# Small products in fewer bursts in the attention and the scan of a hybrid layer

## The chip, the core and the metric

The kernel runs on one core of a Trainium2 chip. The metric is the time on the device in microseconds (us), lower is better; a kernel is run several times and the median counts. The engines of the core work side by side, each through its own list of instructions in order: TensorE (PE in the profile; its weight loads are PEld), VectorE (DVE), ScalarE (ACT), GpSimd (POOL) and SyncE (SP), which issues transfers. An instruction that needs what another engine makes waits on a semaphore, and all that stands behind it in its list waits with it.

## What is computed

One layer over 2048 tokens of width 1024 and 16 learned meta tokens. One combined projection feeds two branches. Branch A is a gated DeltaNet (8 heads of 128, chunks of 64 in the reference, 128 in the kernel); branch B is a sliding-window attention in which four query heads share each of four key heads, over the own chunk of 64, the two before it and the meta tokens.

```python
def step(S, inp):                                   # branch A, the scan over chunks
    u_c, w_c, attn_c, q_c, k_c, gl_c = inp
    v_new = u_c - jnp.einsum('bhik,bhkv->bhiv', w_c, S)
    o_c = jnp.einsum('bhik,bhkv->bhiv', q_c, S) + jnp.einsum('bhij,bhjv->bhiv', attn_c, v_new)
    S = S * gl_c[..., None, None] + jnp.einsum('bhik,bhiv->bhkv', k_c, v_new)
    return S, o_c
...
scores = jnp.einsum('bkgncd,bknsd->bkgncs', q, k_w).astype(f32) * (SWA_HD ** -0.5)   # branch B
scores = scores - slopes[:, :, None, None, None] * dist
probs = jax.nn.softmax(jnp.concatenate([scores, sink], axis=-1), axis=-1)[..., :-1]
o = jnp.einsum('bkgncs,bknsd->bkgncd', probs.astype(v_w.dtype), v_w)
...
y_a = o_a * silu(z_a)                               # after a root mean square norm per head
y_b = o_b * silu(z_b)
mixed = g_a * (y_a @ w_proj_a) + g_b * (y_b @ w_proj_b)
return layer_norm(DEEPNORM_ALPHA * h + mixed @ w_out, ln_w, ln_b)
```

## The kernel before

The tokens are worked through in four blocks of 512. The bulk of the work is the projections: for each unit of 128 output columns a function issues 24 big products (L311, 128 x 512) into one bank of PSUM; the products use a high and a low part of the data and of the weights, which ScalarE (L275, the cast) and VectorE or GpSimd (L146, the difference) make from each weight tile.

Between the big products stands everything else. After six big products a projection yields; `run()` then advances a clock by one *tick* and gives each of two streams at most one step, at the rates in `RATES` and `SIDE`. A unit is thus four ticks. The stream `chain` holds the scan of four head groups (`stage_c`) and then the attention (`swa()`); `side` prepares the groups (decays, the key products of `stage_b1`, the triangular inverses). A step that has a tail (an evaluation that waits for another engine) hands it to `bg()`, a heap of background tasks: `yield 2` in a task lets it go on two ticks later, and a tick releases the due tasks ahead of the streams' steps. The order of each engine's list comes from this and from nothing else. On TensorE the small products of a step so form a *burst* between big ones.

The attention works through 16 items a block (key head `kv`, a pair of chunks `cp2`):

- `swa_front` issues eight score products (L1105), four operations on VectorE that add the position penalty and keep the minimum (L1107, each followed by a row that reads the accumulator), and m2, the sink's share (L1110). A background task does the exponentials on ScalarE two ticks later (L1117, L1119), and three ticks after these the normalisation on VectorE: sum L1121, reciprocal L1122, four scalings L1126.
- `swa_turn(ch, w)` transposes the probabilities of one of two chunks (L1140); ScalarE copies them out, rounded, as the high part (L1142), and a tick later VectorE makes the low part (L1147).
- `swa_vals(ch, w)` multiplies them with the values (L1156, L1158 with the low part, L1159). `swa_out` adds the two halves of the result (ScalarE L1164, VectorE L1165) and gates it into `zs` (L1169, two operations).

The front of the next item is issued one step ahead of the transposes of an item, and an item's second value products and its output (`late`) in the steps of the next one. In the scan, per chunk: the product of keys and state (L971), then the right-hand side, the triangular solve, `wd` (L984), its product into the state; `out` multiplies the chunk's attention matrix with `wd` (L960), adds (L962) and squares (L965). At the end a reciprocal square root of the square sums (L1001 and the helper lines L160 to L169), eight scales (L1006), and the output transposes of `stage_y` (L1023).

## Time and profile before

| | us |
|---|---|
| median of 3 runs (2647.66 to 2649.97) | 2648.5 |
| the profiled execution's own time | 2648.3 |
| its span, first to last instruction | 2646.5 |
| TensorE busy | 2608.6 (99%) |
| VectorE busy | 1533.4 (58%) |
| ScalarE busy | 1222.9 (46%) |
| GpSimd busy | 772.8 (29%) |

Durations below come from the profiled execution. A matmul's end is modelled in it and neighbouring matmuls overlap, so what a product adds is read from the start of one to the start of the next, or from the chain that ended last. x4 in a row is a group of four neighbouring instructions of one kind. The mean granted clock of TensorE was 0.998 of full speed.

### The profile page before, as it was taken

How to read it: one execution, taken by the hardware profiler on the slowest of the kernel's cores; microseconds unless marked ns; L12 is line 12 of the kernel's file. 1: busy time of each engine (PE TensorE's matmuls, PEld its weight loads, DVE VectorE, ACT ScalarE, POOL GpSimd, SP SyncE). 2: the span in 40 equal slices, each digit the busy share in tenths (PEclk: the TensorE clock that was granted, in tenths of full speed). 3: DMA queues.
4: the chain of work that ended last, by engine and by line, in shares of the span. 5: the costliest groups of instructions: out<-in, count | busy, mean ns of one | idle time of the engine just before them, and what ended most of it. 6: DMA issues, size and time to landing. Idle time of an engine off the chain costs nothing.

```text
span 2646.5 us, 44333 instructions
## 1 busy us (share of the span) xinstructions
PE 2608.6 (99%) x15444; PEld 2173.8 (82%) x15444; DVE 1533.4 (58%) x3863; ACT 1222.9 (46%) x3260; POOL 772.8 (29%) x1792
## 2 busy tenths in 40 slices
PE   9999999999999999999999999999999999999998
PEld 7677878888888888888888888888888888888886
DVE  6667756763565554763465554676347456476435
ACT  4565545552245544653224554565323454365422
POOL 2554333532056330111116532010102753011022
PEclk9999999999999999999999999999999999999999
DMA  7655555653675454674466545476347644557533
GB/s 257 207 198 180 186 191 159 200 167 96 205 244 169 135 167 143 201 207 132 152 225 186 170 135 164 151 212 184 120 157 243 190 142 149 164 172 210 171 98 136
DMA packets 243136, 461.61 MB, mean 174 GB/s; under 512 B 77648, under 2 KB 135760, under 8 KB 242912
## 3 DMA queue, kind: packets, MB, share of 16 engines
q1 hardware_dynamic: 242912, 458.78, 54.4%
q8 instruction: 122, 2.00, 0.3%
q14 instruction: 102, 0.84, 0.1%
HBM read 379.87 MB, written 78.81 MB: 173 GB/s over the span
## 4 chain that ended last, share of the span: by engine, by line
PE 89%; DVE 6%; ACT 3%; DMA 1%; issue 1%; SPq 0%; POOL 0%; DVEq 0%; ACTq 0%
PE acc L311 63%; PE ps L1140 2%; PE ps L1105 2%; PE ps L915 1%; PE ps L960 1%; PE ps L807 1%; PE ps L971 1%; PE ps L1158 1%; PE ps L992 1%; PE acc L1408 1%; PE acc L1411 1%; PE acc L1410 1%; PE ps L979 1%; PE ps L981 1%; PE ps L1408 1%; PE ps L1411 1%
## 5 line engine op out<-in xcount | busy, mean ns | idle before, releaser
L311 PE MATMUL acc<-xh,wh 128*128 128x512 f32 x1800 | 735.2, 408 | 0.3 <-ACT wh L275 0.3
L311 PE MATMUL acc<-xl,wh 128*128 128x512 f32 x1800 | 705.4, 392 | 0.0
L311 PE MATMUL acc<-xh,wl 128*128 128x512 f32 x1800 | 480.7, 397 | 0.0
L275 ACT ACTIVATE wh<-wr 128x1024 fp32r<-128x1024 f32 (+1 forms) x246 | 258.4, 1050 | 281.6 <-PE acc L311 151.8
L311 PEld LDWEIGHTS acc<-xh,wh 128*128 128x128 f32 x1800 | 339.1, 188 | 60.1 <-issue 1.4
L311 PEld LDWEIGHTS acc<-xl,wh 128*128 128x128 f32 x1800 | 339.7, 189 | 57.1
L311 PEld LDWEIGHTS acc<-xh,wl 128*128 128x128 f32 x1800 | 329.1, 189 | 65.6 <-issue 0.5
L718 DVE SCALAR_TENSOR_TENSOR s<-st,cw,s 128x512 f32<-128x512 f32 x288 | 229.4, 797 | 108.2 <-ACT st L713 101.2
L311 PE MATMUL acc<-y,wh 128*128 128x512 f32 x1024 | 251.5, 392 | 0.0
L146 DVE TENSOR_TENSOR wl<-wr,wh 128x1024 fp32r<-128x1024 f32 (+2 forms) x125 | 161.9, 1295 | 149.7 <-ACT wh L275 128.6
L841 POOL TENSOR_TENSOR tm<-X,g 128x60 f32<-128x60 f32 (+24 forms) x496 | 163.1, 329 | 251.8 <-DMA g<-d 216.7
L311 PEld LDWEIGHTS acc<-y,wh 128*128 128x128 f32 x1024 | 188.5, 188 | 36.7
L311 PE MATMUL acc<-xh,wr 128*128 128x512 f32 x624 | 210.7, 402 | 0.0
L1257 POOL TENSOR_TENSOR g<-g 128x512 f32<-128x512 f32 x32 | 69.7, 2177 | 395.4 <-DVE g L1250 385.5
L843 POOL TENSOR_TENSOR X<-X,tm 128x60 f32<-128x60 f32 (+24 forms) x496 | 170.8, 344 | 38.8
L1142 ACT ACTIVATE s<-ps 104x512 fp32r<-104x512 f32 (+2 forms) x128 | 76.3, 597 | 153.3 <-PE ps L1140 137.3
L1250 DVE SCALAR_TENSOR_TENSOR g<-g,acc 128x512 f32<-128x512 f32 x64 | 44.0, 687 | 154.5 <-PE acc L311 154.5
L311 PEld LDWEIGHTS acc<-xh,wr 128*128 128x128 f32 x624 | 115.6, 188 | 21.5
L311 PE MATMUL acc<-y,wl 128*128 128x512 f32 x512 | 130.7, 392 | 0.0
L146 POOL TENSOR_TENSOR wl<-wr,wh 128x256 fp32r<-128x256 f32 x120 | 87.0, 756 | 137.4 <-ACT wh L275 116.6
L760 POOL TENSOR_TENSOR g<-cm,gh 128x256 fp32r<-128x256 f32 x64 | 53.9, 872 | 249.6 <-DVE gh L672 206.9
L1241 ACT ACTIVATE g<-acc,bg__162 128x512 f32<-128x512 f32 x64 | 44.1, 689 | 177.3 <-PE acc L311 171.0
(340 smaller groups left out, 4679.6 us busy)
## 6 DMA issues: line engine op xcount, KB each, us to landing
wr<-in_wfm_dram SPq DMA_DIRECT2D x214, 512.0 KB
wl<-ws SPq DMA_DIRECT2D x165, 512.0 KB
wr<-ws SPq DMA_DIRECT2D x78, 512.0 KB
wh<-ws SPq DMA_DIRECT2D x75, 512.0 KB
ws<-wl SPq DMA_DIRECT2D x68, 512.0 KB
g<-kd SPq DMA_DIRECT2D x240, 96.0 KB
ws<-wh SPq DMA_DIRECT2D x38, 512.0 KB
wr<-in_wo_dram SPq DMA_DIRECT2D x32, 512.0 KB
```

Source lines behind the costliest of these rows:

```text
L146: eng.tensor_tensor(out=out_, in0=src, in1=f(hi), op=ALU.subtract)
L275: A.activation(hi[:, k], raw[:, k], AF.Copy)
L311: T.matmul(ps, w_[:, k, :], r_(k), start=(n == 0), stop=(n == 3 * NK - 1))
L718: V.scalar_tensor_tensor(out=acc, in0=st[:, 3 - d:TB + 3 - d], scalar=cw[:, s, 3 - d:4 - d], in1=acc, op0=ALU.mult, op1=ALU.add)
L760: G.tensor_tensor(out=gt[:, hh, c:c + 2], in0=tri.unsqueeze(1).to_broadcast([P, 2, P]), in1=part[:, c:c + 2, h0 + hh:h0 + hh + 1].to_broad ...
L841: G.tensor_tensor(out=tm[:, :n, :r], in0=X[:, :n, j:j + 1].to_broadcast([P, n, r]), in1=L[:, j:j + 1, j + 1:].to_broadcast([P, n, r]), op= ...
L843: G.tensor_tensor(out=X[:, :n, j + 1:], in0=X[:, :n, j + 1:], in1=tm[:, :n, :r], op=ALU.add)
L1105: T.matmul(o_, d["q", rt][:, 2 * cp2 + ch], KX[:, l, ch, s:208], start=l == 0, stop=l == 1)
L1140: T.transpose(out=pT[0:kt, j * 256 + rt * P:j * 256 + rt * P + P], in_=Pt[:, ch, rt, s + j * kt:s + j * kt + kt], identity=ident)
L1142: A.activation(ph[0:kt], pT[0:kt], AF.Copy)
L1257: G.tensor_tensor(out=m[:, u % 2, :], in0=t[:, 0, :], in1=t[:, 1, :], op=ALU.add)
L1408: T.matmul(acc, ah, wl[:, k2, :], start=False, stop=kq == 3 and k2 == 1)
```

## The change

In the attention an item has three steps in place of five: the first transposes and the late value products of the item before go in one step, the second transposes and the first value products in another; the low part counts as ready a tick later. In the scan the product of `out` is issued in the step that starts the next chunk, behind the product of keys and state, and the last one ahead of the attention. The key products of `stage_b1` form two bursts instead of one, the output transposes wait three ticks instead of one, a meta triangle's first step one tick more; two copies of the meta keys stand ahead of the differences. A rate changes from 1.20 to 1.00. The numbers of small and of big products are the same.

```diff
--- before.py
+++ after.py
@@ -44,7 +44,7 @@
 
 GS = (26, 9)
 NG = 6
-RATES = (0.45, 0.45, 0.45, 0.50, 1.20)
+RATES = (0.45, 0.45, 0.45, 0.50, 1.00)
 SIDE = (0.60, 0.50, 0.50, 0.55, 0.35)
 
 
@@ -398,10 +398,11 @@
     def meta_kb(u):
         def go(pf):
             for i in range(2):
+                for a in (0, 64):
+                    A.activation(kmt[a:a + 64, 0, 2 * u + i, :], pf[64 * i:64 * i + 64, :NM], AF.Copy)
+            for i in range(2):
                 kv = 2 * u + i
                 src = pf[64 * i:64 * i + 64, :NM]
-                A.activation(kmt[0:64, 0, kv, :], src, AF.Copy)
-                A.activation(kmt[64:128, 0, kv, :], src, AF.Copy)
                 for a in (0, 64):
                     V.tensor_tensor(out=kmt[a:a + 64, 1, kv, :], in0=src, in1=f(kmt[64 * i:64 * i + 64, 0, kv, :]), op=ALU.subtract)
         return go
@@ -490,7 +491,7 @@
             for hh in range(2):
                 T.matmul(pz[:NM, hh * NM:hh * NM + NM], M[:, lv, hh, :], W[:, 1, hh, :], start=True, stop=True)
             A.activation(Z, pz[:NM, 0:32].rearrange("p (h i) -> p h i", h=2), AF.Copy)
-            yield 2
+            yield 2 + (g == 0)
             n = 2 if lv < 3 else 1
             pw = bank()
             for hh in range(2):
@@ -800,19 +801,20 @@
             yield from until(lambda: "E" in d)
             E = d["E"]
             yield
-            pks = [bank() for hh in range(2)]
-            for hh in range(2):
-                for c in range(NC4):
-                    kc = kT[:, hh, c * P:(c + 1) * P]
-                    T.matmul(pks[hh][:, c * P:(c + 1) * P], kc, kc, start=True, stop=True)
             V.tensor_scalar(out=sk, in0=sk, scalar1=4e-6, scalar2=None, op0=ALU.add)
             V.reciprocal(out=cj, in_=sk)
             V.tensor_tensor(out=cj, in0=cj, in1=beta[:, :, h0:h0 + 2].rearrange("p c h -> p h c"), op=ALU.mult)
             V.tensor_scalar(out=ncj, in0=cj, scalar1=-1.0, scalar2=None, op0=ALU.mult)
             V.tensor_tensor(out=ce, in0=cj, in1=eg[:, 1, :, h0:h0 + 2].rearrange("p c h -> p h c"), op=ALU.mult)
             for hh in range(2):
+                pk = bank()
                 for c in range(NC4):
-                    V.scalar_tensor_tensor(out=LT[:, hh * NC4 + c, :], in0=pks[hh][:, c * P:(c + 1) * P], scalar=ncj[:, hh, c:c + 1],
+                    kc = kT[:, hh, c * P:(c + 1) * P]
+                    T.matmul(pk[:, c * P:(c + 1) * P], kc, kc, start=True, stop=True)
+                if hh:
+                    yield
+                for c in range(NC4):
+                    V.scalar_tensor_tensor(out=LT[:, hh * NC4 + c, :], in0=pk[:, c * P:(c + 1) * P], scalar=ncj[:, hh, c:c + 1],
                                            in1=E[:, hh, c * P:(c + 1) * P], op0=ALU.mult, op1=ALU.mult)
             d.update(ktok=ktok, LT=LT, sk=sk, cj=cj, ce=ce)
             bg(inverse(g))
@@ -954,21 +956,27 @@
             so = tiny([P, 2, NC4], "so")
 
             def out(c, wd):
-                yield 2
-                pks = bank()
+                po = bank()
                 for hh in range(2):
-                    T.matmul(pks[:, hh * P:hh * P + P], attn[:, hh, c, :], wd[:, 0, hh, :], start=True, stop=True)
-                yield 2
-                V.tensor_tensor(out=o[:, :, c, :], in0=pks[:, 0:256].rearrange("p (h d) -> p h d", h=2), in1=o[:, :, c, :], op=ALU.add)
-                yield 1
-                for hh in range(2):
-                    A.activation(junk, o[:, hh, c, :], AF.Square, accum_out=so[:, hh, c:c + 1])
-                d["so", c] = True
-
+                    T.matmul(po[:, hh * P:hh * P + P], attn[:, hh, c, :], wd[:, 0, hh, :], start=True, stop=True)
+
+                def end():
+                    yield 2
+                    V.tensor_tensor(out=o[:, :, c, :], in0=po[:, 0:256].rearrange("p (h d) -> p h d", h=2), in1=o[:, :, c, :], op=ALU.add)
+                    yield 1
+                    for hh in range(2):
+                        A.activation(junk, o[:, hh, c, :], AF.Square, accum_out=so[:, hh, c:c + 1])
+                    d["so", c] = True
+
+                bg(end())
+
+            wd = None
             for c in range(NC4):
                 pks = bank()
                 for hh in range(2):
                     T.matmul(pks[:, hh * P:hh * P + P], kT[:, hh, c * P:(c + 1) * P], S[g][:, hh, :], start=True, stop=True)
+                if c:
+                    out(c - 1, wd)
                 R = s2([P, 2, P])
                 for hh in range(2):
                     V.scalar_tensor_tensor(out=R[:, hh, :], in0=pks[:, hh * P:hh * P + P], scalar=neg[:, c, h0 + hh:h0 + hh + 1],
@@ -993,8 +1001,8 @@
                 for hh in range(2):
                     V.scalar_tensor_tensor(out=S[g][:, hh, :], in0=S[g][:, hh, :], scalar=eg[:, 2, c, h0 + hh:h0 + hh + 1],
                                            in1=pu[:, hh * P:hh * P + P], op0=ALU.mult, op1=ALU.add)
-                bg(out(c, wd))
                 yield
+            out(NC4 - 1, wd)
 
             def end():
                 yield lambda: ("so", NC4 - 1) in d
@@ -1014,7 +1022,7 @@
 
             d = gr[g]
             yield lambda: ("ok", "zs", 1) in d
-            yield 1
+            yield 3
             o, zs = d["o"], d["zs"]
             gr[g] = None
             for hh in range(2):
@@ -1145,6 +1153,7 @@
                 yield 1
                 pl = s2([P, 512], F32R)
                 V.tensor_tensor(out=pl[0:kt], in0=pT[0:kt], in1=f(ph[0:kt]), op=ALU.subtract)
+                yield 1
                 w["p", ch] = kt, ph, pl
 
             bg(end())
@@ -1209,13 +1218,11 @@
                     yield
                 yield from until(lambda: w["n"])
                 swa_turn(0, w)
-                yield
                 if late is not None:
                     late()
-                    yield
-                swa_turn(1, w)
                 yield
                 yield from until(lambda: ("p", 0) in w and ("ok", "zs", 1) in sr[kv])
+                swa_turn(1, w)
                 w["pO"] = bank()
                 swa_vals(0, w)
                 yield
```

What this does to the order of instructions at three places, from the two programs' printed order; a name's number tells one buffer from another. TensorE, block 2, attention before: two of the four score rows of an item (ps_12746; its probabilities will be g_12735), six big products, and the first transposes of the item before, whose probabilities are g_12615.

```order
L1105 MATMUL ps_12746<-g_12596,g_11697 128x208 x2
L1105 MATMUL ps_12746<-g_12596,g_11823 128x208 x2
L311 MATMUL acc_12760<-xh_7832,wh_12650 128x512
L311 MATMUL acc_12760<-xl_7833,wh_12650 128x512
L311 MATMUL acc_12760<-xh_7832,wh_12650 128x512
L311 MATMUL acc_12760<-xl_7833,wh_12650 128x512
L311 MATMUL acc_12760<-xh_7870,wh_12650 128x512
L311 MATMUL acc_12760<-xl_7871,wh_12650 128x512
L1140 MATMUL ps_12767<-cm,g_12615 104x128 x4
L311 MATMUL acc_12760<-xh_7870,wh_12650 128x512
```

After, at the same item:

```order
L1113 MATMUL ps_13281<-g_13137,g_12083 128x208 x2
L1113 MATMUL ps_13281<-g_13137,g_12205 128x208 x2
L311 MATMUL acc_13295<-xh_7832,wh_13177 128x512
L311 MATMUL acc_13295<-xl_7833,wh_13177 128x512
L311 MATMUL acc_13295<-xh_7832,wh_13177 128x512
L311 MATMUL acc_13295<-xl_7833,wh_13177 128x512
L311 MATMUL acc_13295<-xh_7870,wh_13177 128x512
L311 MATMUL acc_13295<-xl_7871,wh_13177 128x512
L1148 MATMUL ps_13308<-cm,g_13156 104x128 x4
L1165 MATMUL ps_13236<-s_13234,s_12908 128x4x64
L1167 MATMUL ps_13236<-s_13249,s_12908 64x4x64 x2
L1168 MATMUL ps_13236<-s_13234,s_12908 128x4x64
```

The transposes (now L1148) still stand six big products behind the scores (L1113) of the next item; the three rows of value products that follow them (ps_13236) are those of the item before, which had a place of their own.

VectorE, block 1, before: the normalisation of an item (g_6416) and the four bias-and-minimum operations of the next (g_6556), which the list calls ISA.

```order
L1121 TENSOR_TENSOR ls_6419<-ls_6419,m_1191_6418 128x4
L1122 RECIPROCAL ls_6419<-ls_6419 128x4
L1126 TENSOR_SCALAR g_6416<-g_6416,ls_6419 128x208 x4
L1107 ISA g_6556,mn_6557<-ps_6560,g_6019,nsnk 128x208
L1107 ISA mn_6557 128x1
L1107 ISA g_6556,mn_6557<-ps_6560,g_6019,nsnk 128x208
L1107 ISA mn_6557 128x1
L1107 ISA g_6556,mn_6557<-ps_6567,g_6019,nsnk 128x208
L1107 ISA mn_6557 128x1
L1107 ISA g_6556,mn_6557<-ps_6567,g_6019,nsnk 128x208
L1107 ISA mn_6557 128x1
L1110 TENSOR_TENSOR m_1220_6558<-mn_6557,snk 128x4
```

VectorE after, block 2, at the TensorE rows shown above: g_13270 is the next item, g_13156 the one whose transposes are issued next.

```order
L1115 ISA g_13270,mn_13271<-ps_13274,g_13022,nsnk 128x208
L1115 ISA mn_13271 128x1
L1115 ISA g_13270,mn_13271<-ps_13274,g_13022,nsnk 128x208
L1115 ISA mn_13271 128x1
L1115 ISA g_13270,mn_13271<-ps_13281,g_13022,nsnk 128x208
L1115 ISA mn_13271 128x1
L1115 ISA g_13270,mn_13271<-ps_13281,g_13022,nsnk 128x208
L1115 ISA mn_13271 128x1
L1118 TENSOR_TENSOR m_2343_13272<-mn_13271,snk 128x4
L1129 TENSOR_TENSOR ls_13159<-ls_13159,m_2321_13158 128x4
L1130 RECIPROCAL ls_13159<-ls_13159 128x4
L1134 TENSOR_SCALAR g_13156<-g_13156,ls_13159 128x208 x4
```

The normalisation stood ahead of the next item's four operations and m2; now it stands behind them. This is so for items 2 to 14 of each block.

VectorE, start of the attention of block 2, before: m2 of the second item, the addition of the scan's last `out` (L962), the normalisation of the items 0 (g_11749) and 1, a low part, and then the first of the square-root steps.

```order
L1110 TENSOR_TENSOR m_2062_11800<-mn_11799,snk 128x4
L962 TENSOR_TENSOR g_10778<-ps_11774,g_10778 128x2x128
L1047 SCALAR_TENSOR_TENSOR g_11823<-acc_11724,g_11823 64x8x64 x2
L1121 TENSOR_TENSOR ls_11752<-ls_11752,m_2052_11751 128x4
L1122 RECIPROCAL ls_11752<-ls_11752 128x4
L1126 TENSOR_SCALAR g_11749<-g_11749,ls_11752 128x208 x4
L1121 TENSOR_TENSOR ls_11801<-ls_11801,m_2062_11800 128x4
L1122 RECIPROCAL ls_11801<-ls_11801 128x4
L1126 TENSOR_SCALAR g_11798<-g_11798,ls_11801 128x208 x4
L1147 TENSOR_TENSOR s_11893<-ps_11872,s_11877 104x512
L1001 SCALAR_TENSOR_TENSOR so_11517<-so_11517,sq_10559 128x8
```

After, the square-root steps' end, the scales (now L1014) and the same two normalisations:

```order
L167 SCALAR_TENSOR_TENSOR rst_11879<-so_11543,ro_11875 128x8
L168 TENSOR_TENSOR rst_11879<-rst_11879,ro_11875 128x8
L169 SCALAR_TENSOR_TENSOR ro_11875<-rst_11879,ro_11875 128x8
L1014 TENSOR_SCALAR g_10801<-g_10801,ro_11875 128x128 x8
L1129 TENSOR_TENSOR ls_11772<-ls_11772,m_2054_11771 128x4
L1130 RECIPROCAL ls_11772<-ls_11772 128x4
L1134 TENSOR_SCALAR g_11769<-g_11769,ls_11772 128x208 x4
L1129 TENSOR_TENSOR ls_11825<-ls_11825,m_2067_11824 128x4
L1130 RECIPROCAL ls_11825<-ls_11825 128x4
L1134 TENSOR_SCALAR g_11822<-g_11822,ls_11825 128x208 x4
```

The square-root steps and the scales moved from behind both normalisations to a place ahead of them.

VectorE after, in one item behind the end of each of three key heads: behind the normalisation stand the output's addition and gatings (L1174, L1178), a split of the branch's output (L146), the first low part (L1155), a gate and the second low part.

```order
L1134 TENSOR_SCALAR g_13270<-g_13270,ls_13273 128x208 x4
L1174 TENSOR_TENSOR s_13434<-ps_13350,s_13434 64x512
L1178 TENSOR_TENSOR g_12440<-s_13434,g_12440 64x2x128 x2
L146 TENSOR_TENSOR y_13445<-g_11963,y_13362 128x1024
L1155 TENSOR_TENSOR s_13452<-ps_13423,s_13428 104x512
L1257 SCALAR_TENSOR_TENSOR g_13247<-g_13247,acc_13410 128x512
L1155 TENSOR_TENSOR s_13479<-ps_13460,s_13465 104x512
```

## Rows read from the trace of the kernel before

**Rows 1.** The page: busy time and share of the span by engine.

```profile
PE 2608.6 (99%) x15444; PEld 2173.8 (82%) x15444; DVE 1533.4 (58%) x3863; ACT 1222.9 (46%) x3260; POOL 772.8 (29%) x1792
```

**Rows 2.** TensorE's waits by releaser over the span: us in total, times, longest.

```profile
PE ps L1158 <- DVE s L1147: 2.6, 5, 1.6
...
PE ps L1140 <- DVE g L1126: 1.4, 5, 0.3
```

**Rows 3.** Chain that ended last, block 2, attention: start us, us, what.

```profile
1745.22 0.12 PE ps L1156
1745.34 0.23 PE ps L1158 x2
...
1747.09 0.88 PE ps L1105 x8
1747.97 1.40 PE acc L311 x6
1749.37 0.44 PE ps L1140 x4
```

**Rows 4.** Timeline of VectorE, block 2, attention: start us, us, engine, line, operation.

```profile
1744.92 0.69 DVE L732 SCALAR_TENSOR_TENSOR g<-s,acc 128x512 f32<-128x512 f32 x1
...
1746.13 0.15 DVE L1121 TENSOR_TENSOR ls<-ls,m 128x4 f32<-128x4 f32 x1
...
1746.53 1.04 DVE L1126 TENSOR_SCALAR g<-g,ls 128x208 f32<-128x208 f32 x4
1747.67 0.43 DVE L1107 CUSTOM_DVE_ANT_0 g<-ps,g,nsnk 128x208 f32<-128x208 f32 x1
...
1749.21 0.16 DVE L1110 TENSOR_TENSOR m<-mn,snk 128x4 f32<-128x4 f32 x1
1749.29 0.68 DVE L732 SCALAR_TENSOR_TENSOR g<-s,acc 128x512 f32<-128x512 f32 x1
1749.89 1.22 DVE L146 TENSOR_TENSOR y<-g,y 128x1024 fp32r<-128x1024 f32 x1
1751.02 0.68 DVE L1147 TENSOR_TENSOR s<-ps,s 104x512 fp32r<-104x512 f32 x1
```

**Rows 5.** Timeline of TensorE in the same stretch.

```profile
1746.93 1.04 PE L1105 MATMUL ps<-g,g 128*128 128x208 f32 x8
...
1749.21 0.60 PE L1140 MATMUL ps<-cm,g 128*104 128x128 f32 x4
```

**Rows 6.** Timeline of ScalarE in the same stretch: the output's upper half.

```profile
1742.69 0.59 ACT L1164 ACTIVATE s<-ps 64x512 f32<-64x512 f32 x1
```

**Rows 7.** Timeline of TensorE, block 0: two bursts of transposes that touch.

```profile
439.48 0.60 PE L1023 MATMUL ps<-cm,g 128*128 128x128 f32 x4
439.92 0.60 PE L1140 MATMUL ps<-cm,g 128*104 128x128 f32 x4
```

**Rows 8.** Timeline of ScalarE, block 2, first items of the attention.

```profile
1696.58 1.20 ACT L1043 ACTIVATE g<-acc 64x512 fp32r<-64x512 f32 x2 [3.40 <-PE acc L311]
...
1699.59 1.05 ACT L275 ACTIVATE wh<-wr 128x1024 fp32r<-128x1024 f32 x1
1700.54 0.46 ACT L1117 ACTIVATE g<-g,mn 128x208 f32<-128x208 f32 x1
...
1702.44 0.30 ACT L965 ACTIVATE junk<-g 128x128 f32<-128x128 f32 x1
...
1703.30 0.60 ACT L1142 ACTIVATE s<-ps 104x512 fp32r<-104x512 f32 x1
```

**Rows 9.** Timeline of VectorE behind it: square-root steps, scales, low part.

```profile
1704.66 0.15 DVE L1001 SCALAR_TENSOR_TENSOR so<-so,sq 128x8 f32<-128x8 f32 x1
...
1708.65 0.68 DVE L1147 TENSOR_TENSOR s<-ps,s 104x512 fp32r<-104x512 f32 x1
```

**Rows 10.** Windows: us, busy (count) by engine, PEclk the granted clock.

```profile
433.90:437.20 3.30, 3.30 (x10) 2.50 (x9) 2.92 (x17) 0.00 (x0) 0.30 (x2) 0.50 0.88 289
1548.00:1552.00 4.00, 2.97 (x16) 2.21 (x15) 3.25 (x6) 1.30 (x5) 0.00 (x0) 1.00 0.43 136
```

## The prediction

> **What bounds the kernel now.** I read the page first. TensorE is busy for 2608.6 us of the 2646.5 us span, 99% [rows 1]; VectorE has 58% and ScalarE 46%. A number of products that stays the same therefore leaves only two ways to move the time: what a product costs, and how long TensorE stands still. The list of TensorE's waits came next: the two that belong to the attention are 2.6 and 1.4 us in the whole span [rows 2]. So small a sum says that in the kernel before, every small product finds its operand ready; the order is loose enough. Then I followed one attention item in the chain that ended last [rows 3]: a burst of eight score products 0.88, six big products 1.40, four transposes 0.44, six big products, one set of value products 0.12 + 0.23 + 0.12. Nothing but TensorE stands in it. The question is thus whether the new order is still loose. For that I set the program order of VectorE (shown with the change) beside the durations of VectorE's own timeline in the same stretch [rows 4].
>
> **The change, part by part.**
>
> *Fewer bursts.* Both kernels issue the same products; in the printed order the small ones stand in 760 bursts between big products before and in 632 after, 128 fewer. What a boundary costs can be read where two bursts already touch: four transposes of L1023 start at 439.48, the four of L1140 right behind them at 439.92, 0.44 later [rows 7]. A lone burst of four adds 0.44 to the chain as well, at 1749.37 [rows 3]. So merging saves nothing that the rows resolve; half of their last digit, 0.005 a boundary, gives **-0.6 us**. The Trainium skill would pay more: "TensorE: Matmul & The Clock Gate", section "Back-to-back issue gap", gives some 81 ns for each 128-column product in a sustained stream. Four would be 0.32, and if the other 0.12 were the price of a burst's ends, 128 of them would give 15 us back, an estimate from that page; the touching pair in rows 7 speaks against it.
>
> *The attention's period.* An item took five ticks, it now takes four (a tick is six big products). Its probabilities are normalised by a background task that runs 2 + 3 = 5 ticks after its scores. With a period of five the task fell due in the tick of the next item's scores and, being released ahead of the chain, stood before their four bias-and-minimum operations on VectorE. With four it falls due one tick after them: VectorE first does the next item's four, then m2, then the sum, reciprocal and four scalings. The first transposes of the old item follow the new item's scores on TensorE by only six big products in both orders, but what they need now lies behind all of that.
>
> The price, from F, the start of the scores at 1746.93 [rows 5]. The first bias operation starts at F + 0.74, m2 at F + 2.28, the next VectorE operation 0.08 later [rows 4], so the sum can start at F + 2.36. From sum to first scaling is 1746.13 to 1746.53, 0.40; two scalings, which the first transposes need, are half of 1.04 [rows 4]. They end at F + 3.28; with another 0.08 to hand over, F + 3.36. TensorE is there at 1749.21, F + 2.28 [rows 5]. It waits **1.08 us**. The printed order has this pattern for items 2 to 14 of each block, 13 x 4 = 52 places: **+56.2 us**. The bounds: if VectorE reaches the first bias operation 0.2 earlier, now that no scalings stand before it, 0.88 or 46 us; if what VectorE does for the item before (its low parts) still runs at F + 0.74, each 0.1 us adds 5.2 us, and one low part (0.68) half over would make it 74. I take the middle row. Nothing fills these waits: TensorE works in order, and behind the transposes stand only big products that could have gone ahead.
>
> *Low part moved behind the value products.* The transposes of the first half and the late value products of the item before now go in one burst. The low part (L1155) of that half then stands on VectorE behind the output's addition and two gatings, which wait for those value products. From the start of the transposes: 0.44 + 0.47 to the end of the values, about 0.2 to ScalarE's copy (an estimate: half the scores, 0.44, are done 0.30 before the first bias operation at 0.74), 1742.69 to 1744.92 from that copy to the next free slot of VectorE, 2.23 [rows 4, 6], low part 0.68: 4.02. TensorE asks for it after 0.44 + 0.47 + twelve big products 2.80 + 0.44 + 0.12 = 4.27 [rows 3]. A margin of 0.25 remains, so this is free while nothing else comes between. In three places a block VectorE does (the split at L146, 1749.89 to 1751.02, 1.13 [rows 4]): 1.13 - 0.25 = 0.88, times 12 is **+10.6 us**. Below, that is nothing if the split comes early; above, see the rivals. The extra step before the low part counts as ready costs no more: it is the third of four ticks, and hidden by the twelve big products.
>
> *Start of the attention.* The last output product of the scan is now issued right before the attention, so its square sums, the square-root steps and the eight scales stand ahead of the first normalisation. On ScalarE, behind the first scores: two q copies 1.20, squares 0.86 (1702.44 to 1703.30), a weight cast 0.95 (1699.59 to 1700.54), two sets of exponentials of 1.90 (1700.54 to 1702.44), squares 0.86 [rows 8], together 7.67. Then on VectorE the steps and scales, 1704.66 to 1708.65, 3.99 [rows 9], and sum to second scaling 0.92 + 0.08: 12.66 behind the first scores. TensorE is there after 0.88 + 1.40 + 0.88 + 4 x 1.40 = 8.76 [rows 3]. A wait of 3.9, once a block: **+15.6 us**; none if ScalarE's list is 4 us earlier than I set it.
>
> *The rest.* Waits of the old attention steps that may vanish: at most 2.6 + 1.4 [rows 2], **-4.0 us**. In the scan the output product moves beside another small product and has the same cover of big ones behind it. The decay products in two bursts, the output transposes two ticks later, the meta triangle's extra tick and the order of the meta copies: all lie in background tasks, hidden by the ticks of big products they are spread over; if that cover were gone they would show as new waits of the size of those in rows 2, a few us. The rate 1.20 to 1.00 does nothing, as a stream takes at most one step a tick either way. VectorE does not become the bound: per item it loses idle time only, 58% before.
>
> The sum: 56.2 + 10.6 + 15.6 - 4.0 - 0.6 = **+77.8**. The profiled execution took 2648.3 us (span 2646.5 and 1.8 around it), 0.2 under the median 2648.5. 2648.3 + 77.8 = **2726 us**.
>
> **The rivals.**
> A, as summed: 2726, its own range 2705 to 2746.
> B, only the normalisation wait is real: the split comes early enough and ScalarE's list at the start is ahead. 2648.3 + 56.2 - 4.6 = 2700. For it: idle time on both engines; against it: an in-order list gives no credit for idle time in other places.
> C, the low part is late in every item, not in 12 places. One weight cast (0.95, rows 8) and one split fall in each four ticks, so once an item; whichever of them comes between takes the 0.25 margin. Half a us in the 52 places, +26: 2752. For it: the thin margin; against it: the printed order has the split there only three times a block.
> D, the waits take the clock along. Between 433.90 and 437.20 TensorE was busy all the time with a granted clock of 0.50, that is 1.2 GHz of 2.4, right behind the wait of 1.6 for a low part [rows 2, 10]; half of 3.30 lost at each of 52 waits is +86: 2812. Against it: around 1550 TensorE stood still for 1.03 of 4.00 us and the clock stayed at 1.00 [rows 10]. The Trainium skill tells of such a case ("TensorE: Matmul & The Clock Gate", section "A second HAM failure mode: psum-queue depth-cycling"): short frequent idling between groups made the clock go up and down. Rows 10 show both outcomes.
> E, the other side, faster: a burst has a toll after all. Four transposes at a big product's pace would be 4 x 128/512 x 1.40/6 = 0.23 instead of 0.44 [rows 3]; were the rest, 0.21, due to the burst's ends, 128 fewer give 27 back: 2621, provided that the transposes' wait is nearly nil. It decides from a wait under 0.5 us a place (27/52). Against it: rows 7, and 1.08 us of VectorE work in the printed order.
> F, no change: burst toll and waits cancel, or the scalings run ahead.
>
> **How the numbers follow.** A 0.60, B 0.17, C 0.11, D 0.05, E 0.05, F 0.02. The likeliest, 2726, is the prediction. 2688 to 2754 takes in A, C and B with B's lower bound (46 instead of 56 us, 2690), some 0.85, leaving out D, E, F. A measurement of this kernel can't tell 0.2% (5 us) from no change; below that by more: E, 0.05; within: F, 0.02; above: 0.93.
>
> **What would show it.** In TensorE's waits after: L1148 for L1134 some 50 times, about 1 us each, 50 to 60 us; in the four longest 3 to 4 us behind L1014; L1167 for L1155 a dozen times. TensorE's busy time stays near 2609 and its share falls to 96 or 97%. On VectorE's timeline L1134 starts some 0.5 behind L1118. I am wrong if L1134 is found before L1115, if these waits are under 0.3 us, or if TensorE's busy time falls by 10 us or more.

## The result, and the profile after

The changed kernel takes 2838.05 us (median of 6 runs, 2833.62 to 2842.7), before 2648.53 in the same comparison: a ratio of 1.0716, 95% interval 1.0702 to 1.073. It is slower, as forecast, but by 189.5 us and not by 77.8. The page of the profile after, span and busy times:

```profile
span 2840.9 us, 44396 instructions
PE 2660.5 (94%) x15444; PEld 2206.0 (78%) x15444; DVE 1535.9 (54%) x3863; ACT 1223.8 (43%) x3260; POOL 776.5 (27%) x1792
```

The profiled execution is the slowest of the six, 2842.7 us; its span grew by 194.4 us. TensorE's busy time, which should have stayed, grew by 51.9 against [rows 1]; the other 142.5 are standstill. Its mean granted clock over the span is 0.980, before 0.998. The list of TensorE's waits (us in total, times, longest) says what it stood still for:

```profile
PE ps L1148 <- DVE g L1134: 104.7, 56, 9.4
PE acc L311 <- DMA wh<-ws: 19.6, 3, 7.8
PE ps L1167 <- DVE s L1155: 9.4, 10, 1.0
PE ps L792 <- DVE g L724: 6.5, 7, 1.1
```

The first row is the wait that was forecast, the third the low part's; the second, a wait for weights on their way by transfer, was costed at nothing. One item of block 1 on TensorE, to be laid beside [rows 5]:

```profile
1206.26 1.04 PE L1113 MATMUL ps<-g,g 128*128 128x208 f32 x8
...
1208.07 0.39 PE L311 MATMUL acc<-xh,wh 128*128 128x512 f32 x1
1208.30 0.39 PE L311 MATMUL acc<-xl,wh 128*128 128x512 f32 x1
1209.50 0.68 PE L1148 MATMUL ps<-cm,g 128*104 128x128 f32 x4 [0.82 <-DVE g L1134]
```

The same item on VectorE, to be laid beside [rows 4]:

```profile
1207.00 0.43 DVE L1115 CUSTOM_DVE_ANT_0 g<-ps,g,nsnk 128x208 f32<-128x208 f32 x1 [0.85 <-PE ps L1113]
...
1208.55 0.16 DVE L1118 TENSOR_TENSOR m<-mn,snk 128x4 f32<-128x4 f32 x1
1208.62 0.15 DVE L1129 TENSOR_TENSOR ls<-ls,m 128x4 f32<-128x4 f32 x1
...
1209.03 1.04 DVE L1134 TENSOR_SCALAR g<-g,ls 128x208 f32<-128x208 f32 x4
```

From the start of the scores: bias operations at 0.74, sum at 2.36, scalings at 2.77, transposes at 3.24. The working had 0.74, 2.36, 2.76 and 3.36. The record of a big product lasts 0.39, though the next one starts 0.23 behind it; so of the 0.97 that TensorE loses here (1208.30 to 1209.50, less 0.23) only 0.82 is listed as a wait, and 0.15 counts as busy time. But block 0 is another picture. TensorE there:

```profile
553.19 1.04 PE L1113 MATMUL ps<-g,g 128*128 128x208 f32 x8
...
559.62 0.60 PE L1148 MATMUL ps<-cm,g 128*40 128x128 f32 x4 [4.00 <-DVE g L1134]
```

and VectorE's and GpSimd's rows in front of it:

```profile
557.18 0.43 DVE L1115 CUSTOM_DVE_ANT_0 g<-ps,g,nsnk 128x208 f32<-128x208 f32 x1 [4.18 <-POOL g L1094]
```

```profile
553.30 2.81 POOL L146 TENSOR_TENSOR wl<-wr,wh 128x256 fp32r<-128x256 f32 x4 [9.67 <-ACT wh L275]
556.05 0.36 POOL L1086 CAST g<-kmt 128x32 fp32r<-128x32 f32 x2
556.38 0.57 POOL L1089 TENSOR_SCALAR mo<-md 128x16 f32<-128x16 f32 x2
556.91 0.44 POOL L1094 TENSOR_TENSOR g<-mo,slp 128x32 f32<-128x32 f32 x2
```

The bias operations start 3.99 behind the scores, since they need the bias columns of the meta tokens (L1094). GpSimd makes these only behind a weight split (L146), and the split waits for ScalarE's cast. In TensorE's waits, by stretches, the 104.7 us are: block 0 57.8 in 14 waits, 9.4 of them the first; blocks 1 to 3 3.2 for the first item and 12.4 to 12.5 for 13 others each.

The granted clock completes it. Windows (us, busy time by engine in the order PE, PEld, DVE, ACT, POOL, then PEclk, the granted clock): the attention of block 0 and that of block 1, each without its first wait:

```profile
457.00:640.00 183.00, 136.88 (x651) 112.22 (x651) 84.33 (x268) 70.41 (x186) 53.38 (x133) 0.87 0.37 117
```

```profile
1175.00:1320.00 145.00, 129.10 (x726) 106.63 (x724) 96.57 (x301) 80.50 (x204) 15.84 (x70) 1.00 0.58 174
```

With waits of 1 us in each item the clock stayed at 1.00; with waits of 4 us it was at 0.50 for a stretch behind each.

Not all of the 51.9 us of busy time are the clock. TensorE was busy for some 91 us at a granted clock of 0.50 in this execution and for 3 in the one before; half of the difference, some 44 us, is lost to the clock, 25 of it in the attention of block 0 (estimates from the clock's records in the two traces). The other 8 are about what the waits add at 0.15 each by breaking the overlap of neighbouring products (an estimate: TensorE stands still in some 60 more places than before).

### The profile page after: what moved, and what is told of

Same layout as the page of the kernel before. It is cut to its first block, busy times and chain, and to the rows that moved or that the text cites. A ratio compares the mean times of both kernels' runs of the same rounds, so it can differ in the third digit from the quotient of the medians.

```text
span 2840.9 us, 44396 instructions
## 1 busy us (share of the span) xinstructions
PE 2660.5 (94%) x15444; PEld 2206.0 (78%) x15444; DVE 1535.9 (54%) x3863; ACT 1223.8 (43%) x3260; POOL 776.5 (27%) x1792
## 4 chain that ended last, share of the span: by engine, by line
PE 58%; DVE 8%; POOL 3%; ACT 3%; DMA 2%; issue 2%; SPq 1%; DVEq 0%; ACTq 0%; POOLq 0%
PE acc L311 41%; DVE g L1115 2%; PE ps L1148 2%; POOL X L845 1%; POOL tm L843 1%; PE acc L1418 1%; PE acc L1415 1%; PE acc L1417 1%; PE ps L1167 1%; DVE s L719 1%; DMA g<-d 1%; PE ps L1418 1%; PE ps L1415 1%; PE ps L1417 1%; PE ps L987 1%
## 5 line engine op out<-in xcount | busy, mean ns | idle before, releaser
L311 PE MATMUL acc<-xh,wh 128*128 128x512 f32 x1800 | 742.8, 413 | 19.7 <-DMA wh<-ws 19.6
L311 PE MATMUL acc<-xl,wh 128*128 128x512 f32 x1800 | 717.8, 399 | 0.0
L311 PEld LDWEIGHTS acc<-xh,wh 128*128 128x128 f32 x1800 | 346.8, 193 | 85.3 <-issue 21.8
L311 PEld LDWEIGHTS acc<-xl,wh 128*128 128x128 f32 x1800 | 347.8, 193 | 60.9
L311 PEld LDWEIGHTS acc<-xh,wl 128*128 128x128 f32 x1800 | 337.9, 192 | 69.8 <-issue 0.9
L843 POOL TENSOR_TENSOR tm<-X,g 128x60 f32<-128x60 f32 (+24 forms) x496 | 169.1, 341 | 298.8 <-DMA g<-d 263.6
L146 DVE TENSOR_TENSOR wl<-wr,wh 128x1024 fp32r<-128x1024 f32 (+2 forms) x125 | 163.4, 1307 | 157.9 <-ACT wh L275 136.7
L1148 PE MATMUL ps<-cm,g 128*104 128x128 f32 (+2 forms) x512 | 85.7, 291 | 104.8 <-DVE g L1134 104.7
L1148 PEld LDWEIGHTS ps<-cm,g 128*104 128x104 f32 (+2 forms) x512 | 59.2, 132 | 140.7 <-issue 106.2
L146 POOL TENSOR_TENSOR wl<-wr,wh 128x256 fp32r<-128x256 f32 x120 | 85.3, 742 | 239.0 <-ACT wh L275 229.0
L1115 DVE CUSTOM_DVE_ANT_0 g<-ps,g,nsnk 128x208 f32<-128x208 f32 (+2 forms) x256 | 94.2, 425 | 99.0 <-POOL g L1094 58.1
```

Of the source, the lines that this page charges most:

```text
L146: eng.tensor_tensor(out=out_, in0=src, in1=f(hi), op=ALU.subtract)
L311: T.matmul(ps, w_[:, k, :], r_(k), start=(n == 0), stop=(n == 3 * NK - 1))
L843: G.tensor_tensor(out=tm[:, :n, :r], in0=X[:, :n, j:j + 1].to_broadcast([P, n, r]), in1=L[:, j:j + 1, j + 1:].to_broadcast([P, n, r]), op= ...
L1115: V.tensor_tensor_reduce(out=Pt[:, ch, rt, s:208], in0=pS[:, rt * 256 + s:rt * 256 + 208], in1=bias[:, ch, rt, s:208], scale=1.0, scalar=n ...
L1148: T.transpose(out=pT[0:kt, j * 256 + rt * P:j * 256 + rt * P + P], in_=Pt[:, ch, rt, s + j * kt:s + j * kt + kt], identity=ident)
```

## The experiments

All times are medians; the kernel before took 2647.8 to 2649.7 beside them, and differences are to it unless another kernel is named.

**First four: which part, which order.** `attn_only` is the kernel before with the edits of `swa()` and `swa_turn` alone.

> The kernel before with the attention's part of the change alone (three steps an item, the low part counted ready a tick later). Order theory: nearly all of the 189 us comes from the normalisation standing behind the next item's bias operations, so 2780 to 2805; the waits of L1140 for L1126 fill 80 to 105 us, the granted clock falls in block 0's attention only. Rival, the scan and the key products carry much of it: under 2750.

Measured: 2749.4 (1.0379, 1.0364 to 1.0395), +100 and not the 130 to 155 of the order theory. Its waits:

```profile
PE ps L1140 <- DVE g L1126: 63.9, 64, 2.2
PE ps L1159 <- DVE s L1147: 23.6, 32, 1.6
```

The normalisation is late in all four blocks, by 14.5 us in 13 waits in block 1 and by 20.4 us in 25 in block 0, and the low part makes most of the rest. `rest_only` is the change without those edits.

> The change without the attention's part. Order theory: 2675 to 2695, the rest being the waits for weights at the start of blocks 1 to 3 (some 8 us each) and some 10 us in block 0; no waits of the transposes for the normalisation beyond before's 1.4 us. Rival, the scan and the key products carry much of it: 2740 or more.

Measured: 2703.8 (1.0213, 1.0196 to 1.0231), +54, between the two. Its waits:

```profile
PE ps L1148 <- DVE g L1134: 19.9, 6, 9.4
PE acc L311 <- DMA wh<-ws: 14.7, 3, 5.2
```

The first is the start of the attention in each block, the second the weights. The two parts make 154 of 189 us; 35 come only where both are present. `norm_earlier` is the whole change with

```diff
                 A.activation(m2, m2, AF.Exp)
-                yield 3
+                yield 2
```

and a condition that holds the step with the first transposes and the late value products until these have their low part.

> The whole change, but the normalisation falls due two ticks after the exponentials instead of three, so that it stands ahead of the next item's bias operations again. Order theory: the transposes' waits vanish (under 10 us in all), the clock stays up in block 0, 2680 to 2700. Rival, an item of four ticks is too short whatever the order (low part, exponentials or outputs late, new waits take over): 2740 or more.

Measured: 2753.1 (1.0394, 1.0377 to 1.0412). The order theory fell here, by over 50 us. And as the items of block 0 also stand at another place in their unit, behind the 24th big product from the third item on and not the 6th, part of the 85 us that this kernel wins against the change is not the order's (see `shift_block0`). The waits moved on in part instead of vanishing; of the second row 22.9 are the first item's in each block:

```profile
PE ps L1167 <- DVE s L1155: 26.8, 19, 1.9
PE ps L1148 <- DVE g L1134: 23.8, 6, 9.2
```

`bias_early`:

```diff
-                    swa_bias(k2, ld[0][3])
+                    if i == 0:
+                        swa_bias(k2, ld[0][3])
                     nxt = swa_front(*seqn[i + 1], *ld.pop(0))
+                    if ld:
+                        swa_bias(seqn[i + 2][0], ld[0][3])
```

> The whole change, but GpSimd's bias of the item after next is issued right behind an item's scores, ahead of the next weight split on GpSimd. Order theory: in block 0 the first bias operation of VectorE starts 0.7 us behind the scores instead of 3.9, the waits there fall from 4 to 1 us in a dozen places (36 us), the clock comes back with them (20 to 30 us): 2770 to 2790; blocks 1 to 3 unchanged. Rival, block 0 is slow because of something else (weights arriving, the clock by itself): over 2825.

Measured: 2782.2 (1.0505, 1.0486 to 1.0525), 56 us less than the change. TensorE's waits in its block 0 (430 to 640), and a window of its attention there:

```profile
PE ps L1148 <- DVE g L1134: 22.1, 15, 9.4
```

```profile
457.00:610.00 153.00, 136.78 (x754) 111.42 (x754) 100.61 (x301) 79.48 (x205) 60.80 (x141) 1.00 0.51 154
```

Without the first, 9.4, that is 0.9 a wait instead of 3.7, and the clock is at 1.00. So block 0's excess, some 4 us an item instead of 1, is GpSimd's bias behind the split.

**Second four: the parts of the rest, and block 0 another way.** `b1_only`, `scan_only` and `small_only` are the kernel before with the hunk of `stage_b1`, the hunks of the scan, and the other small edits (rate, meta copies, meta triangle, output transposes). `shift_block0` is the whole change with

```diff
+            for _ in range(3 if b == 0 else 0):
+                yield
             swa_bias(0, ld[0][3])
```

> The kernel before with the key products in two bursts alone. If the side stream's extra step is what makes the decay matrices, the inverse and with it the weights queued on SyncE late, the weights' waits of the big products (three times 5 us) are here, and some us in block 0: 2665 to 2685. If those waits come of the scan's new order: 2646 to 2652.

Measured: 2683.9 (1.0141, 1.0124 to 1.0158), +36.

> The kernel before with the scan's part alone. If the last output product ahead of the attention puts square-root steps and scales before the first normalisation, L1140 waits for L1126 once a block, 9 us in block 0 and 3 in the others, 17 to 20 in all: 2664 to 2672. If that wait needs the other parts too: under 2656.

Measured: 2686.3 (1.0143, 1.0126 to 1.016), +38.5, twice what was expected: the first transposes wait 7.1 to 7.4 us in each block, where the whole change has 9.4 in block 0 and 3.2 in the others. The attention's steps are not the reason, since `rest_only` has the old ones as well, and waits of 9.4 and 3.2.

```profile
PE ps L1146 <- DVE g L1132: 32.6, 11, 7.4
```

> The kernel before with the rate, the meta copies, the meta triangle's tick and the output transposes' ticks alone. Background work under cover: 2646 to 2652. If the output transposes' two ticks push VectorE's and ScalarE's work into the attention: over 2655.

Measured: 2654.0 (1.0022, 1.0013 to 1.0032), +6, between the two.

> The whole change with three idle steps ahead of the attention in block 0, so that its items' scores stand behind the 24th big product of a unit instead of the 6th, as in blocks 1 to 3. If GpSimd's split, released at a unit's start, makes block 0 slow, this takes the transposes' waits there from 4 to 1 us and keeps the clock up, like the earlier bias: 2770 to 2790. If block 0 is slow for another reason: over 2825.

Measured: 2785.8 (1.0522, 1.0506 to 1.0537), as `bias_early`. Its waits between 430 and 640:

```profile
PE ps L1148 <- DVE g L1134: 21.6, 22, 3.1
```

This covers the 35 us that neither part has alone, and more: with block 0 shifted the whole change costs 138, less than the 154 of its parts. In the printed order the scores stand after 6, 12, 18 and 24 big products of a unit in turn before the change, since an item has five ticks and a unit four. With four ticks an item keeps one place for the whole block, from the third item on. In block 0 that is after the 6th in the change, right behind the split that is released at a unit's start, and after the 24th in `attn_only` and in `shift_block0`. The rest of the change moved the attention's start and so chose the bad place.

**Third four: each part mended.** `attn_mended` is `attn_only` with the normalisation a tick earlier (the edit of `norm_earlier`) and

```diff
                 swa_turn(0, w)
-                if late is not None:
-                    late()
                 yield
...
                 swa_turn(1, w)
+                if late is not None:
+                    late()
                 w["pO"] = bank()
```

> The kernel before with the attention's part alone, of which two places are moved: the normalisation falls due a tick earlier (ahead of the next item's bias operations), and the late value products with their output go into the step of the second transposes (behind the first low part). Order theory: an item of four ticks with four bursts fewer costs nothing once the order is right, 2644 to 2656, waits of the transposes and the low part under 10 us in all. If a burst's ends had a toll of 0.2 us: 2625 to 2640. If four ticks are too short for VectorE's chain: 2665 or more.

Measured: 2750.4 (1.0388, 1.0374 to 1.0402): nothing won against `attn_only`, though the order is mended. Its waits, and one item on TensorE and VectorE:

```profile
PE ps L1140 <- DVE s L1147: 56.4, 52, 2.4
```

```profile
1151.94 1.04 PE L1105 MATMUL ps<-g,g 128*128 128x208 f32 x8
...
1154.98 0.64 PE L1140 MATMUL ps<-cm,g 128*104 128x128 f32 x4 [0.62 <-DVE s L1147]
```

```profile
1151.27 0.68 DVE L1166 TENSOR_TENSOR s<-ps,s 64x512 f32<-64x512 f32 x1 [3.79 <-ACT s L1165]
1151.99 0.85 DVE L1170 TENSOR_TENSOR g<-s,g 64x256 f32<-64x256 f32 x2
...
1153.29 1.04 DVE L1126 TENSOR_SCALAR g<-g,ls 128x208 f32<-128x208 f32 x4
1154.25 0.68 DVE L1147 TENSOR_TENSOR s<-ps,s 104x512 fp32r<-104x512 f32 x1
```

Transposes read no low part. They wait for it because they write into the bank that it still reads: the small products have four banks in turn (the pool `pp` in the kernel), and an item takes five. VectorE does the output, the scalings and the low part one after the other, and ends at 1154.9, 3 us behind the next item's scores. In each of the three orders tried with four ticks something on this chain is late: the normalisation and the low part in `attn_only`, the low part in `norm_earlier`, the bank here.

`scan_scales_later` is `scan_only` with `bg(end(), 8)` for `bg(end(), 1)` ahead of `stage_y`.

> The scan's part alone, its square-root steps and scales set off seven ticks later, so that the first two normalisations of the attention stand ahead of them. Theory: the wait of 7 us at the start of the attention in each block vanishes, 2645 to 2655. If the scan's new order loses by its own products and additions: still over 2670.

Measured: 2670.5 (1.0083, 1.007 to 1.0097), +22.6, more than expected; the start of the attention is mended (2.3 us of those waits left), but other waits came in the scan (L791 for L723 9.4 us, L985 for L980 8.2). `b1_late_store` is `b1_only` with

```diff
-DMA = (1, 3, 4, 1, 2, 7)
+DMA = (1, 3, 4, 5, 2, 7)
```

> The key products in two bursts alone, with the store of the inverse's diagonal blocks placed four ticks later in SyncE's queue. If the weights wait behind that store, which waits for GpSimd's inverse, the wait for weights (5.5 us in the profile of the two bursts alone) goes and with it the loss at the start of blocks 1 to 3 (7 to 8 us each): 2655 to 2668. If the loss has other causes: within 6 us of 2684.

Measured: 2649.4 (1.0007, 0.9998 to 1.0016): the whole loss of the key products is gone, more than expected. In the change, SyncE's queue (SPq) stands 17.7 us at the store that waits for GpSimd's inverse, between 840 and 915, where it stood 6.9 before, and the weights stand behind it. The change and the kernel before:

```profile
SPq L851 <- POOL X L845: 17.7, 1, 17.7
SPq L849 <- POOL X L843: 6.9, 1, 6.9
```

The same between 740 and 900 in `b1_only`, where a wait of 5.5 us for weights follows on TensorE, and in `b1_late_store`, where none does:

```profile
SPq L850 <- POOL X L844: 20.2, 2, 14.6
SPq L850 <- POOL X L844: 9.1, 2, 7.2
```

What TensorE does behind such a wait, in the change:

```profile
907.63 0.77 PE L311 MATMUL acc<-xh,wh 128*128 128x512 f32 x1 [7.80 <-DMA wh<-ws]
908.20 0.63 PE L311 MATMUL acc<-xl,wh 128*128 128x512 f32 x1
908.62 0.63 PE L311 MATMUL acc<-xh,wh 128*128 128x512 f32 x1
```

The products behind the wait follow each other at 0.42 us instead of 0.23: the granted clock is 0.50 there, the lower of the two. `all_mended` is the whole change with `bias_early`, `attn_mended`'s moves, the later scales and the later store.

> The whole change with all the moves together: normalisation earlier, late value products in the second step, GpSimd's bias earlier, scales later, store later. The order theory has 2650 to 2680 (what is left are waits of block 0 behind the key products); a version that beats the kernel before would be under 2645. If the parts' losses don't come from these places: over 2720.

Measured: 2736.4 (1.0338, 1.0324 to 1.0352), +88, the second outcome; 52.5 us of it is again the transposes' wait for the low part's bank.

**Last three: period or bursts.** `attn_period5` is `attn_only` with an idle step at the end of each item, all its bursts merged as in the change:

```diff
                 swa_vals(0, w)
                 yield
+                if i + 2 < len(seqn):
+                    yield
```

> The attention's part alone with an idle step at the end of each item: the merged bursts stay, but an item takes five ticks again, the normalisation falls due in the tick of the next item's scores, and the phase moves through the unit as before. If the shorter period makes the loss (VectorE's chain and the four small banks have a tick less): 2644 to 2660, waits of transposes and low part under 15 us in all. If the merged bursts themselves make it: over 2700. A toll on each burst's ends would show as 2625 to 2640.

Measured: 2670.1 (1.0088, 1.0074 to 1.0102). This is above the 2660 of the first case and far below the second: of +100 us +22 stay, with no wait for the normalisation among the longer ones:

```profile
PE ps L1159 <- DVE s L1147: 18.3, 23, 3.2
```

By the starts of the same big products in the two profiled executions (spans 2664.9 and 2646.5), 17.8 us fall into the attention of block 0, where 14.8 of the waits above are, and 3.6 into blocks 1 to 3 together, as much as their waits for the low part (1.2 a block); up to block 0's attention this execution is 3.0 ahead. Blocks 1 to 3 have 90 of the 120 bursts that this kernel has fewer. By the same measure the attention of each of these blocks loses 26 us in the change, 24 to 26 in `attn_only`, 29 in `attn_mended`, 14 to 18 in `norm_earlier` and 1.3 to 1.5 here. Five ticks also put the normalisation back ahead of the next item's bias operations; that this order alone isn't enough, `attn_mended` shows. `scan_scales_g3` delays the scales of the last head group only: `bg(end(), 8 if g == 3 else 1)`.

> The scan's part alone, with the scales set off later in the last head group alone, whose scales stand at the start of the attention. If the 22 us that were left with later scales in all groups come from the first three groups' scales in a new place: 2646 to 2655. If they belong to the scan's new order: 2665 to 2675.

Measured: 2651.4 (1.0011, 1.0002 to 1.0019): of 38.5 us 3.5 stay. `full_mended5` is the whole change with five ticks, the later store and the last group's later scales.

> The whole change with five ticks an item, the inverse's store four ticks later and the last group's scales later. Were the three places the whole loss: 2645 to 2665, the 6 us of the small edits among it. A version faster than the kernel before: under 2643. Otherwise, parts that disturb each other: over 2680.

Measured: 2688.3 (1.0148, 1.0134 to 1.0162), +40. The parts alone make 22 + 1.5 + 3.5 + 6 = 33; the other 7 come only where they stand together. Among this kernel's waits are 13.2 us of the triangular solve (L987) for its right-hand side on VectorE (L982), 5.1 in the change; why was not looked for. No version beat the kernel before.

## Why the prediction was right in direction and wrong in size

*Bound, and bursts at nothing: right.* No kernel with fewer bursts gained where its waits were gone; `attn_period5` merges and stays level in blocks 1 to 3. Rival E (0.21 us for a burst's ends) would have given 19 us back there for 90 bursts; 3.6 were lost, and the waits for the low part account for them.

*The normalisation's wait, "13 x 4 = 52 places: +56.2 us": right mechanism, right price in three blocks, wrong price in block 0.* In the 39 places of blocks 1 to 3 it measured 37.3 us, 0.96 each against 1.08. The first failing step is that one item of block 2 stood for block 0 too. There the 13 places cost 48.4, 3.7 each, because the first bias operation doesn't follow the scores by 0.74 but waits for GpSimd. What would have told was on GpSimd's list in block 0 before, a split just ahead of the bias (there L1086):

```profile
465.61 3.03 POOL L146 TENSOR_TENSOR wl<-wr,wh 128x256 fp32r<-128x256 f32 x4 [4.41 <-ACT wh L275]
...
469.46 0.44 POOL L1086 TENSOR_TENSOR g<-mo,slp 128x32 f32<-128x32 f32 x2
```

Together with an item as long as a unit this means that every item can meet the split at the same place. The bound that I set there (74 us, for low parts in the way) was the wrong mechanism and still too low: 37.3 + 48.4 = 85.7.

*"TensorE's busy time stays near 2609": the second failing step, and by size the largest.* The sum has no term for it; it grew by 51.9 us at equal work, to 2660.5, some 44 of it by the clock (an estimate, above). Case D (0.05, 86 us) had named the clock, but with a wrong condition. Not each wait took it: the waits of 1 us left it at 1.00, as the row around 1550 said [rows 10], those of 4 us in block 0 didn't, and neither did those for weights. `bias_early` gives 56 us back where 57.8 - 22.1 = 36 us of waits went; the other 20 are busy time (2638.7 instead of 2660.5), with the clock back at 1.00 in that stretch.

*"Hidden by the ticks of big products", and if not, "a few us": the third failing step.* The key products in two bursts cost 36 us alone. What I didn't count is SyncE's queue: the decay matrices, the inverse's transfers and the weights stand in one list, and GpSimd's inverse, later in relation to it, held the weights. `b1_late_store` takes the store out of the weights' way and the loss is gone. The small edits cost 6 more.

*Start of the attention, +15.6:* 9.4 + 3 x 3.2 = 19.0 measured. The mechanism is right, with the scales (L1014) ahead of the first normalisation, but that the sum is near is partly luck: 9.4 and 3.2 stand for 3.9 each. *Low part, +10.6 in 12 places:* 9.4 in 10 places, near; what the merged step left of margin, 0.25, was as thin as said, since `norm_earlier` made it 26.8.

*The sum in the trace:* transposes 104.7 - 1.4, weights 19.6, low part 9.4 - 2.6 and busy time 51.9 make 181.6 of 194.4; the 12.8 left over are small waits, the largest of them L792 for L724, 6.5 against 1.5 before. Of the 117 us by which the span exceeds the forecast, busy time is 52, the transposes' waits 33, and weights and small waits, for which the sum had no term, 32.

*What I believed after the result and had to give up:* that the order of normalisation and bias operations is the cause in itself. `norm_earlier` and `attn_mended` have it right and lose 100 us, the first with the rest of the change in it. The cause of the attention's loss is the item of four ticks: the chain of VectorE and the four banks have a tick less, and the place in the unit stands still. With five ticks four fifths of that loss is gone. No run separates VectorE's chain from the banks; a fifth bank for the small products would have. Open too is why `scan_only` waits 7 us at the start of the attention in blocks 1 to 3 and the whole change 3, and which of the small edits costs the 6 us; neither was tried.

## What to carry to other kernels

Where a loop of products is threaded through other work, its period is a resource: shortening it by merging steps removes cover from every chain that ran in the gaps, and a fix of the order may, as here, only move the wait along the chain. Compare the period with that of the work around it; if they become equal, each pass meets the same neighbour, and the price has to be read in every block, not in one. And for each step that goes later, look through the transfer queue behind it for loads that the busiest engine needs.

## What was not expected of the hardware

Standing still for about 1 us in every 9.4 left TensorE's granted clock at 1.00 over 145 us; standing still for some 4 us in every 14 brought a mean of 0.87 over 183 us, and a single wait of 7.8 us was followed by products at half speed (0.42 for 0.23 us). The length of the wait alone doesn't decide: in `attn_only` one of 2.17 us (to 1114.44) left the clock at 1.00, one of 2.15 (to 1778.86) was followed by products at 0.50, and so was one of 1.6 in the kernel before [rows 10]. In the whole change the clock took some 44 of 194 us (an estimate, above).
